# The mixer's second part: low parts, decay products and sums of squares on VectorE, weighted inputs and halos on ScalarE

## The chip, the cores and the metric

One core of a Trainium2 chip runs the whole program. The metric is the device time of one launch in microseconds. The engines are named as in the profile: PE is TensorE (PEld its weight loads), DVE is VectorE, ACT is ScalarE, POOL is GpSimd, SP issues the transfers.

## The reference

The program computes one block of a streaming encoder on 1024 tokens of width 1024, in float32: a conditioned RMS norm, a mixer that joins a 31-tap convolution path and a Mamba-2 path, a second conditioned norm, a SwiGLU layer, and a last norm. The part that the change touches is the Mamba-2 path with the products around it:

```python
xbc = jax.nn.silu(causal_depthwise_conv(xbc, ssm_conv_w, ssm_conv_b))      # 4 taps, 24 tiles of 128 channels
xs, bm, cm = jnp.split(xbc, [D_INNER, D_INNER + N_GROUPS * D_STATE], axis=-1)
dt = jax.nn.softplus(dt_raw + dt_bias);  a = -jnp.exp(a_log)
# scan over chunks, 32 heads in 4 groups; xk is xs * dt, ak is dt * a
acs = jnp.cumsum(ak, axis=1)
decay = jnp.exp(jnp.where(causal, acs[:, :, None] - acs[:, None, :], -jnp.inf))
cb = jnp.einsum("blgn,bsgn->blsg", ck, bk)
y_diag = jnp.einsum("blsg,blsgj,bsgjp->blgjp", cb, decay, xk)
y_off = jnp.einsum("blgn,bgjpn,blgj->blgjp", ck, state, jnp.exp(acs))
w_in = jnp.exp(last[:, None] - acs)
new_state = state * jnp.exp(last)[..., None, None] + jnp.einsum("bsgn,bsgj,bsgjp->bgjpn", bk, w_in, xk)
y = (y + d_skip * xs) * jax.nn.silu(z);  yg = yg * rsqrt(mean(yg * yg) + eps)
merged = sigmoid(g_conv) * y_conv + sigmoid(g_ssm) * (y @ w_ssm_out);  x = x + gate * (merged @ w_out)
```

## The kernel before

Activations lie as channels by tokens, in tiles of 128 channels by 512 tokens; the 1024 tokens are two halves, `hf` 0 and 1. TensorE multiplies at a format that keeps fewer bits, so each operand is split into a high part (a rounding copy, ScalarE) and a low part (the rest, a subtraction), and a product is three matmuls: high by high, high by low, low by high. A chunk of weights is 128 by 1024; `load_w` fetches it (512 KB, two buffers `wraw`), and `split_w` makes for each half of it the high part `wh` (L164, ScalarE) and the low part `wl` (L166). Which engine makes `wl` is the `eng` argument of `step`, "pool" (GpSimd) where nothing else is said; chunks are fetched three ahead and split two ahead of their use. `mm3` issues the three matmuls as L180, L181 and L182; only L182 reads `wl`.

The first part of the mixer (`phase_a`) and the SwiGLU layer work with seven products in place of eight on quarters of the operands (`Unit`); their own tables say which engine splits what, and they are not touched. The second part of the mixer (`phase_b`) runs from about 650 to 1450 us. In it, the main line is a list of steps, one chunk of weights each: 24 `group` steps (tiles `p`) whose result goes through the 4-tap convolution `conv4`, then gates, `conv_out` (`co`), `smul` (`s`) and `wout` (`wo`). `mm3` calls `tick`, which lets three background generators advance by given rates: `ssd_all` (the scan, for both halves and four groups), the end of the 31-tap convolution with its normalisation (`conv_var`, `conv_norm`), and `ada` (products of the conditioning vector, tiles `wa_m` and `wa_f`). A scheduler then sets the order on each engine from a timeline of its own and the priorities; every engine executes its list in that order, so what waits holds back all that stands behind it.

What the change touches:

- `SumSq` (L303 to L328) adds squares (made by ScalarE, L318) to an accumulator at L322; the engine is GpSimd where the caller names none. In `phase_b` these are `say` (the scan's groups), `sav` and `spare` (variance of the convolution, squares of the new residual).
- `dt_part` makes `wdec`, the decay from a token to the end of its chunk (L465 and L466), 128 tokens by 32 heads for each of four chunks.
- `ssd`: for each chunk four transposes give `px` in PSUM (tokens by 8 heads of 64); VectorE makes `xdt` from it by `dt` (L563), GpSimd makes the weighted inputs `wx` from `xdt` by `wdec` (L569); `next_state` multiplies `wx` on TensorE (L527) and VectorE adds the result to the scaled state (L531), whose scaling is GpSimd's (L522). `Decay` makes `M`, the decay within a chunk: loaded, four ScalarE instructions (L548), an exponential (L550), and the product with `cbm` (L553), which is GpSimd's for the first half and for every second head of the second, and VectorE's for the rest.
- `conv4` (L1081 to L1097) copies the product from PSUM into `pre` (L1088), scales it in place (L1090), adds three taps on VectorE (L1094), and ends with a tanh (L1096) and `xo` (L1097), which frees the PSUM tile. Three columns at the border of the halves are kept in `halo_s` (L1092) and put back in the second half (L1087), both by VectorE.
- `down_rest` names GpSimd for the sum of squares of the first half's output (L1552).

Of the kernel before, what the change touches and what calls it, by code (L numbers as in the profile page):

```python
# [15 lines left out]
T = 512  # L16
NH = 2
KD = 8
# [53 lines left out]
def build(tc, ins, outs):  # L72
# [230 lines left out]
    class SumSq:  # L303


        def __init__(self, name, square=True, eng=None, acc=None, of=None):
            self.name, self.n, self.square, self.eng = name, 0, square, eng or gp
            self.of, self.rest = of, []
            self.acc = acc if acc is not None else stp.tile([P, T], F32, tag="sacc", name="sa" + name, bufs=3)

# [91 lines left out]
    def dt_part(hf, wide, operands):  # L402
# [61 lines left out]
        act(out=etot, in_=pa[:, P:2 * P], func=AF.Exp)  # L464
        vec.tensor_tensor(out=wdec, in0=pa[:, P:2 * P], in1=acs, op=ALU.subtract)  # L465
        act(out=wdec, in_=wdec, func=AF.Exp)  # L466
        yield
        pt = pstile(f"acsT{hf}")
        for c in range(NCK):
# [16 lines left out]
    def ssd(hf, g, D):  # L486
# [47 lines left out]
        class Decay:  # L534
# [15 lines left out]
                act(out=m, in_=m, func=AF.Exp, scale=-1.0)  # L550

            def mul(self, e):
                (gp if e or hf == 0 else vec).tensor_tensor(out=self.M[e], in0=self.M[e], in1=cbm, op=ALU.mult)  # L553

        last = hf == NH - 1
        M = Decay(0)
# [1 line left out]
        for c in range(NCK):  # L558
            px = pstile(f"xT{hf}{g}{c}")
            for j in range(4):  # L560
                nc.tensor.transpose(out=px[:, j * P:(j + 1) * P], in_=xs[j][:, c * P:(c + 1) * P], identity=ident)
            xd = sp.tile([P, T], F32, tag="xdt", name=f"xdt{hf}{g}{c}", bufs=4)
            vec.tensor_tensor(out=v3(xd), in0=v3(px), in1=heads(dt, c, g), op=ALU.mult)  # L563
            xdt.append(xd)
            if c > 0:
                next_state(c - 1, sn)
            if not (last and c == NCK - 1):
                wx = sp.tile([P, T], F32, tag="wx", name=f"wx{hf}{g}{c}", bufs=2)
                gp.tensor_tensor(out=v3(wx), in0=v3(xd), in1=heads(wdec, c, g), op=ALU.mult)  # L569
                wxs.append(wx)  # L570
            if c == 0:
                M.load()
            elif c == 1:
                M.exp(0)
            elif c == 2:
                M.exp(1)
            else:
                M.mul(0)
                M.mul(1)
            yield 1  # L580
            if not (last and c == NCK - 1):
                sn = new_state(c)
            yield 1
# [179 lines left out]

    prog = []

    def step(fn, ch=None, nk=8, eng="pool", pre=()):
        prog.append((ch, nk, eng, fn, pre))

    W8 = list(range(8))
# [311 lines left out]
    def conv4(pt, i, out, hf):  # L1081

        pre = pools["c"].tile([P, T + SW - 1], F32, tag="pre", name=f"pre{hf}_{i}", bufs=2)
        if hf == 0:
            gp.memset(pre[:, 0:SW - 1], 0.0)
        else:
            vec.tensor_copy(out=pre[:, 0:SW - 1], in_=halo_s[:, i, :])  # L1087
        act(out=pre[:, SW - 1:], in_=pt, func=AF.Copy)  # L1088
        wc = lambda k: sw_h[:, i * SW + k:i * SW + k + 1]
        act(out=pt, in_=pt, func=AF.Identity, scale=wc(3), bias=sb_h[:, i:i + 1])  # L1090
        if hf == 0:
            vec.tensor_copy(out=halo_s[:, i, :], in_=pre[:, T:T + SW - 1])  # L1092
        for k in range(3):
            vec.scalar_tensor_tensor(out=pt, in0=pre[:, k:k + T], scalar=wc(k), in1=pt, op0=ALU.mult, op1=ALU.add)  # L1094
        t = pre[:, 0:T]
        act(out=t, in_=pt, func=AF.Tanh)  # L1096
        vec.scalar_tensor_tensor(out=out, in0=t, scalar=1.0, in1=pt, op0=ALU.add, op1=ALU.mult)  # L1097
# [437 lines left out]
    def down_rest(hf):  # L1535
# [11 lines left out]
        for m in range(KD):  # L1547
            def fd(w, m=m):
                pt = mmtile(f"fd{hf}_{m}")
                mm3(pt, w, range(6), LAST[hf])  # L1550
                if m == 0:
                    D["s"] = SumSq(f"x2_{hf}", eng=vec if hf else gp, of=KD)  # L1552
                    D["x2"] = []
                xt = (pools["u"].tile([P, T], F32, tag="g0", name=f"x2_{hf}_{m}", bufs=N_G0) if hf else
                      ev(f"x2_{hf}_{m}"))
# [198 lines left out]
```

## Time and profile before

| | |
|---|---|
| median of 3 runs | 2137.74 us (2136.13 to 2140.61) |
| the profiled execution, its own time | 2132.49 us |
| its span, first to last instruction | 2130.5 us |
| mean granted TensorE clock | 0.967 of full speed |
| busy: PE, DVE, ACT, POOL | 1954.8, 1561.3, 964.2, 1168.1 us |

The profiled execution is 5.25 us shorter than the median of the three runs; a sum made against its own time is carried to the median by adding that. Busy time of TensorE is the union of its matmuls; what it waits for, and in which stretch, says more than the share over the whole span.

### The profile page before, as it was taken

The numbers are of one execution on the slowest core, as the hardware profiler recorded it, in microseconds if no ns is written. First come the engines' busy times: TensorE is split into PE (matmuls) and PEld (weight loads), VectorE is DVE, ScalarE is ACT, GpSimd is POOL, SyncE is SP. The second block draws the span as 40 slices with busy tenths as digits, with TensorE's granted clock in tenths as the row PEclk, the third lists the DMA queues.
The fourth block names the chain that finished last, engine by engine and source line by source line (L and its number), as shares of the span: only waits on it lengthen the run. The fifth ranks groups of instructions, "written<-read, shape, count | busy, mean of one in ns | idle before, by whom it ended". The sixth has DMA issues, their size and how long they took to land.

```text
span 2130.5 us, 26723 instructions
## 1 busy us (share of the span) xinstructions
PE 1954.8 (92%) x8802; PEld 1554.5 (73%) x8802; DVE 1561.3 (73%) x2242; ACT 964.2 (45%) x1792; POOL 1168.1 (55%) x871
## 2 busy tenths in 40 slices
PE   4879999999998889898989899998999999989997
PEld 3668678787876666676767677776888888767776
DVE  8868889958899878959779783758644444598645
ACT  3534444444444747446344653346333333444243
POOL 4568678887885854585655764555333333331410
PEclk9889999999999989999999999999999999999998
DMA  8223132322323967689788786863422222576553
GB/s 321 80 70 113 68 102 84 119 104 74 109 102 135 302 201 247 201 301 290 242 277 271 246 260 218 275 229 109 149 99 77 77 84 89 180 255 215 190 187 119
DMA packets 163818, 365.94 MB, mean 172 GB/s; under 512 B 18728, under 2 KB 19168, under 8 KB 163680
## 3 DMA queue, kind: packets, MB, share of 16 engines
q1 hardware_dynamic: 163680, 364.25, 51.2%
q8 instruction: 69, 1.13, 0.2%
q14 instruction: 69, 0.57, 0.1%
HBM read 281.04 MB, written 83.13 MB: 171 GB/s over the span
## 4 chain that ended last, share of the span: by engine, by line
PE 53%; DVE 23%; DMA 13%; issue 4%; ACT 3%; POOL 3%; SPq 1%; DVEq 0%; POOLq 0%; ACTq 0%
PE uXp L805 12%; PE uXf L805 10%; PE uZp L805 6%; PE uZf L805 5%; PE uYp L805 3%; PE uYf L805 2%; DMA M<-acs_d 2%; PE uXd L805 2%; DMA wa_f<-in 2%; DMA yl<-y_d 1%; DVE wa_m L242 1%; DVE wa_f L242 1%; DVE Hl L211 1%; PE uZd L805 1%; PE fd L180 1%
## 5 line engine op out<-in xcount | busy, mean ns | idle before, releaser
L166 POOL TENSOR_TENSOR wl<-w,wh 128x512 fp32r<-128x512 f32 x198 | 283.4, 1440 | 226.6 <-ACT wh L164 185.6
L164 ACT ACTIVATE wh<-w 128x512 fp32r<-128x512 f32 x232 | 136.8, 606 | 135.4 <-DMA w<-in 60.1
L918 POOL TENSOR_TENSOR fw<-fw,fw 128x512 f32<-128x512 f32 x40 | 58.0, 1450 | 117.5 <-DMA fw<-in 116.8
L548 ACT ACTIVATE M<-M,dt_acs 128x128 f32<-128x128 f32 x256 | 81.0, 390 | 45.2 <-DMA M<-acs_d 45.0
L553 POOL TENSOR_TENSOR M<-M,cbm 128x512 f32<-128x512 f32 x48 | 69.4, 1456 | 44.4 <-ACT M L550 25.9
L660 DVE SCALAR_TENSOR_TENSOR pcM<-u,cw_eo,pcM 128x512 f32<-128x512 f32 x120 | 90.3, 752 | 2.7
L660 DVE SCALAR_TENSOR_TENSOR pcQ<-u,pc,pcQ 128x512 f32<-128x512 f32 x112 | 84.4, 754 | 3.0
L182 PE MATMUL s<-Hh,wl 128*128 128x512 f32 x192 | 77.8, 406 | 3.0 <-POOL wl L166 3.0
L660 DVE SCALAR_TENSOR_TENSOR pcR<-u,pc,pcR 128x512 f32<-128x512 f32 x104 | 78.4, 754 | 2.8
L181 PE MATMUL s<-Hl,wh 128*128 128x512 f32 x192 | 77.1, 401 | 2.5 <-DVE Hl L211 2.5
L180 PE MATMUL s<-Hh,wh 128*128 128x512 f32 x192 | 77.3, 406 | 0.5 <-ACT wh L164 0.5
L916 POOL TENSOR_TENSOR fsf<-fw 128x512 f32<-128x512 f32 x22 | 41.2, 1873 | 65.3 <-DVE cf2l L784 10.8
L180 PE MATMUL p<-Hh,wh 128*128 128x512 f32 x144 | 59.0, 430 | 19.1 <-DVE xo L1097 10.8
L180 PE MATMUL p<-Oh,wh 128*128 128x512 f32 x144 | 60.6, 421 | 8.4 <-DVE xo L1097 8.4
L181 PE MATMUL p<-Hl,wh 128*128 128x512 f32 x144 | 60.7, 423 | 5.9 <-DVE Hl L341 5.9
L985 DVE TENSOR_TENSOR s2f<-s2f,uZf 128x512 f32<-128x512 f32 x22 | 15.1, 687 | 62.5 <-PE uZf L805 62.5
L181 PE MATMUL p<-Ol,wh 128*128 128x512 f32 x144 | 60.0, 417 | 0.0
L182 PE MATMUL p<-Oh,wl 128*128 128x512 f32 x144 | 59.5, 414 | 0.0
L925 POOL TENSOR_TENSOR fw<-fw 128x512 f32<-128x512 f32 x40 | 58.6, 1466 | 1.5
L182 PE MATMUL p<-Hh,wl 128*128 128x512 f32 x136 | 56.8, 418 | 0.0
L1094 DVE SCALAR_TENSOR_TENSOR p<-pre,pc,p 128x512 f32<-128x512 f32 x72 | 53.9, 748 | 0.8 <-ACT p L1090 0.2
L180 PE MATMUL wo<-Oh,wh 128*128 128x512 f32 x128 | 51.6, 403 | 0.0
(3620 smaller groups left out, 6973.7 us busy)
## 6 DMA issues: line engine op xcount, KB each, us to landing
fw<-in SPq DMA_DIRECT2D x133, 512.0 KB, 3.4
w<-in SPq DMA_DIRECT2D x100, 512.0 KB, 4.9
M<-acs_d SPq DMA_DIRECT2D x64, 256.0 KB, 6.1
wa_f<-in SPq DMA_DIRECT2D x48, 256.0 KB, 3.5
wa_m<-in SPq DMA_DIRECT2D x16, 512.0 KB, 10.2
xs<-xbc_d SPq DMA_DIRECT2D x32, 256.0 KB, 5.0
E<-eac_d SPq DMA_DIRECT2D x64, 128.0 KB, 6.1
y<-z_d SPq DMA_DIRECT2D x32, 256.0 KB, 5.2
```

Source lines behind the costliest of these rows:

```text
L164: act(out=hi[:, :n], in_=raw, func=AF.Copy)
L166: eng.tensor_tensor(out=lo[:, :n], in0=raw, in1=hi[:, :n].bitcast(F32), op=ALU.subtract)
L180: nc.tensor.matmul(out=out, lhsT=whi[:, sl], rhs=rh, start=first and i == 0, stop=False)
L181: nc.tensor.matmul(out=out, lhsT=whi[:, sl], rhs=rl, start=False, stop=False)
L182: nc.tensor.matmul(out=out, lhsT=wlo[:, sl], rhs=rh, start=False, stop=last and i == n - 1)
L548: act(out=m[:, sl], in_=m[:, sl], func=AF.Relu, scale=-1.0, bias=acs[:, c * 32 + hd:c * 32 + hd + 1])
L553: (gp if e or hf == 0 else vec).tensor_tensor(out=self.M[e], in0=self.M[e], in1=cbm, op=ALU.mult)
L660: vec.scalar_tensor_tensor(out=pt if k < n - 1 else out or pt, in0=src(k), scalar=w(k), in1=pt, op0=ALU.mult, op1=ALU.add)
L805: nc.tensor.matmul(out=out, lhsT=l[:, sl], rhs=r, start=first and k == 0 and i == 0, stop=k == 3 and i == 2, skip_group_check=True)
L918: e[8].tensor_tensor(out=a21, in0=a11, in1=a21, op=ALU.subtract)
L925: e[10].tensor_tensor(out=a12, in0=a12, in1=a11, op=ALU.subtract)
L1094: vec.scalar_tensor_tensor(out=pt, in0=pre[:, k:k + T], scalar=wc(k), in1=pt, op0=ALU.mult, op1=ALU.add)
```

## The change

Five edits, all of them of who does what; one adds a small product.

1. `step` gives `wl` to VectorE where nothing else is said (188 low parts in the stretch 650 to 1450 us, and those of the two gate chunks near the start, which go through the same default).
2. `Decay.mul` is VectorE's for all 64 tiles (48 of them were GpSimd's).
3. `SumSq` adds on VectorE where no engine is named, and `down_rest` names none.
4. `wx` is made by ScalarE, straight from `px` in PSUM, in eight instructions of 64 columns with the decay as a scale for each partition; `wdec` is multiplied by `dt` once for each half beforehand, since `px` lacks it.
5. The two halo copies of `conv4` are ScalarE's.

```diff
-            self.name, self.n, self.square, self.eng = name, 0, square, eng or gp
+            self.name, self.n, self.square, self.eng = name, 0, square, eng or vec
...
         act(out=wdec, in_=wdec, func=AF.Exp)
+
+        vec.tensor_tensor(out=wdec, in0=wdec, in1=dt, op=ALU.mult)
...
-                (gp if e or hf == 0 else vec).tensor_tensor(out=self.M[e], in0=self.M[e], in1=cbm, op=ALU.mult)
+                vec.tensor_tensor(out=self.M[e], in0=self.M[e], in1=cbm, op=ALU.mult)
...
-                gp.tensor_tensor(out=v3(wx), in0=v3(xd), in1=heads(wdec, c, g), op=ALU.mult)
+                for h in range(J):
+                    hs = slice(h * 64, (h + 1) * 64)
+                    o = c * 32 + g * J + h
+                    act(out=wx[:, hs], in_=px[:, hs], func=AF.Copy, scale=wdec[:, o:o + 1])
...
-    def step(fn, ch=None, nk=8, eng="pool", pre=()):
+    def step(fn, ch=None, nk=8, eng="vec", pre=()):
...
-            vec.tensor_copy(out=pre[:, 0:SW - 1], in_=halo_s[:, i, :])
+            act(out=pre[:, 0:SW - 1], in_=halo_s[:, i, :], func=AF.Copy)
...
-            vec.tensor_copy(out=halo_s[:, i, :], in_=pre[:, T:T + SW - 1])
+            act(out=halo_s[:, i, :], in_=pre[:, T:T + SW - 1], func=AF.Copy)
...
-                    D["s"] = SumSq(f"x2_{hf}", eng=vec if hf else gp, of=KD)
+                    D["s"] = SumSq(f"x2_{hf}", of=KD)
```

Two places show what the scheduler makes of it. The first is on VectorE, at the second chunk `p_21` of the first half's group 2: from its last tap to its `xo`, in the kernel before (`xh_x1m`, `Ol` belong to the next half's normalised input, `ud` to the convolution's variance, `yd` to the scan).

```order
L1094 SCALAR_TENSOR_TENSOR p_21_5999<-pre_22_6052,pc,p_21_5999 128x512
L709 TENSOR_TENSOR ud_7_5762<-ud_7_5762,bcmean_5268 128x512
L1092 COPY halo_s<-pre_8_6130 128x3
L335 SCALAR_TENSOR_TENSOR xh_x1m_5987<-xh_x1m_5987,gmix,bcx1m 128x512
L1094 SCALAR_TENSOR_TENSOR p_22_6078<-pre_8_6130,pc,p_22_6078 128x512
L335 SCALAR_TENSOR_TENSOR xh_x1m_6066<-xh_x1m_6066,gmix,bcx1m 128x512
L335 SCALAR_TENSOR_TENSOR xh_x1m_6144<-xh_x1m_6144,gmix,bcx1m 128x512
L1094 SCALAR_TENSOR_TENSOR p_22_6078<-pre_8_6130,pc,p_22_6078 128x512
L613 SCALAR_TENSOR_TENSOR yd_5907<-xs_2_5372,pc,yd_5907 128x512
L1097 SCALAR_TENSOR_TENSOR xo_6051<-pre_22_6052,p_21_5999 128x512
```

The same place in the changed kernel (its lines stand five further down, L1099 for the taps and L1102 for `xo`; L555 is the product `M`).

```order
L1099 SCALAR_TENSOR_TENSOR p_21_6028<-pre_22_6081,pc,p_21_6028 128x512
L335 SCALAR_TENSOR_TENSOR xh_x1m_6173<-xh_x1m_6173,gmix,bcx1m 128x512
L268 TENSOR_SCALAR vv_5984<-scv_5979 128x4
L606 TENSOR_TENSOR E_6034<-E_6034,yo_6039 128x384
L322 TENSOR_TENSOR say_5675<-say_5675,sqy_1_5877 128x512
L1099 SCALAR_TENSOR_TENSOR p_22_6107<-pre_8_6159,pc,p_22_6107 128x512
L341 SCALAR_TENSOR_TENSOR Ol_5324<-xh_x1m_6016,mod_m,Oh_5323 128x512
L621 TENSOR_TENSOR yd_5936<-E_5888,yd_5936 128x384
L341 SCALAR_TENSOR_TENSOR Ol_5326<-xh_x1m_6095,mod_m,Oh_5325 128x512
L269 TENSOR_SCALAR r_ln_126<-vv_5984 128x4
L166 TENSOR_TENSOR wl_0_6296<-w_6175,wh_0_6294 128x512
L1102 SCALAR_TENSOR_TENSOR xo_6080<-pre_22_6081,p_21_6028 128x512
```

The low part, the sum `say` and the work of the scan now stand between a tap and the `xo` that TensorE waits for. From the chunk's first tap to its `xo` there were 19 other rows on VectorE; now there are 30. From its second tap there were 14; now there are 23.

The second place is the weighted inputs at the start of the scan's first group. On GpSimd they stood, in the kernel before, among low parts and products `M`:

```order
L569 TENSOR_TENSOR wx_5487<-xdt_5482,dt_wdec_2162 128x512
L553 TENSOR_TENSOR M_5447<-M_5447,cbm_5400 128x512
L1085 MEMSET pre_7_5872 128x3
L166 TENSOR_TENSOR wl_4_5813<-w_5707,wh_4_5811 128x512
L553 TENSOR_TENSOR M_5449<-M_5449,cbm_5400 128x512
L166 TENSOR_TENSOR wl_0_5892<-w_5805,wh_0_5890 128x512
```

On ScalarE they stand, in the changed kernel, between the steps of `conv4` (L1093 and L1095 are its copy and its scaling, L1101 its tanh) and the high parts of weights:

```order
L1097 ACTIVATE halo_s<-pre_6_5818 128x3
L164 ACTIVATE wh_0_5919<-w_5834 128x512
L574 ACTIVATE wx_5558<-xT_5548,dt_wdec_2162 128x64 x8
L552 ACTIVATE M_5697<-M_5697 128x512
L164 ACTIVATE wh_4_5923<-w_5834 128x512
L1101 ACTIVATE pre_6_5818<-p_14_5746 128x512
L574 ACTIVATE wx_5603<-xT_5593,dt_wdec_2162 128x64 x8
L1093 ACTIVATE pre_7_5901<-p_15_5844 128x512
```

A block of eight now stands ahead of a tanh, a copy or a high part, where ScalarE had nothing of the kind; GpSimd keeps the scaling of the state and little else in this stretch.

## Rows read from the trace of the kernel before

**Rows 1.** The page, part 1: busy us (share of span) and instructions.

```profile
PE 1954.8 (92%) x8802; PEld 1554.5 (73%) x8802; DVE 1561.3 (73%) x2242; ACT 964.2 (45%) x1792; POOL 1168.1 (55%) x871
```

**Rows 2.** Three stretches: their us, busy us by engine, clock, DMA share, GB/s.

```profile
650.00:900.00 250.00, 216.80 (x1082) 167.51 (x1080) 213.43 (x343) 149.13 (x308) 147.68 (x122) 0.93 0.68 221
900.00:1250.00 350.00, 316.00 (x1656) 246.90 (x1655) 279.85 (x433) 184.13 (x409) 225.68 (x164) 0.96 0.83 273
1250.00:1450.00 200.00, 192.04 (x849) 152.45 (x848) 118.06 (x175) 76.93 (x136) 98.84 (x71) 1.00 0.74 245
```

**Rows 3.** Waits of PE, 650 to 1450 us: total us, times, longest.

```profile
PE p L180 <- DVE xo L1097: 19.2, 3, 10.8
PE yo L596 <- DVE S L531: 8.5, 4, 3.4
PE yd L611 <- POOL M L553: 6.8, 6, 3.6
PE sc L285 <- DVE ry L276: 6.5, 2, 3.5
PE yo L596 <- DVE E L601: 5.6, 3, 3.8
...
PE s L182 <- POOL wl L166: 3.8, 6, 1.2
```

**Rows 4.** Groups on POOL, 650 to 1450 us: busy, mean ns, idle before.

```profile
L166 POOL TENSOR_TENSOR wl<-w,wh 128x512 fp32r<-128x512 f32 x188 | 269.1, 1440 | 198.7 <-ACT wh L164 169.4 <-PE s L182 11.3 <-DMA y_d<-y 9.0
L553 POOL TENSOR_TENSOR M<-M,cbm 128x512 f32<-128x512 f32 x48 | 69.4, 1456 | 44.4 <-ACT M L550 25.9 <-DMA wa_f<-in 12.4 <-DMA E<-eac_d 3.9
L322 POOL TENSOR_TENSOR say<-say,sqy 128x512 f32<-128x512 f32 x24 | 33.5, 1397 | 9.2 <-ACT sqy L318 8.9
L569 POOL TENSOR_TENSOR wx<-xdt,dt_wdec 128x512 f32<-128x512 f32 x28 | 31.3, 1123 | 2.6 <-DVE xdt L563 2.6
```

**Rows 5.** Groups on DVE, 650 to 1450 us.

```profile
L242 DVE CUSTOM_DVE_ANT_0 wa_f<-wa_f,rw,as_f 128x512 f32<-128x512 f32 x24 | 29.0, 1209 | 30.1 <-DMA wa_f<-in 30.1
...
L563 DVE TENSOR_TENSOR xdt<-xT,dt_dt 128x512 f32<-128x512 f32 x32 | 21.2, 681 | 2.9 <-PE xT L561 2.9
...
L1289 DVE TENSOR_TENSOR spl<-spl,mpl 128x512 f32<-128x512 f32 x16 | 18.8, 1177 | 0.3
...
L274 DVE SCALAR_TENSOR_TENSOR ty<-ry 128x4 f32<-128x4 f32 x24 | 11.2, 466 | 0.5
...
L1092 DVE COPY halo_s<-pre 128x3 f32<-128x3 f32 x12 | 5.3, 438 | 6.2 <-ACT pre L1088 6.2
...
L274 DVE SCALAR_TENSOR_TENSOR tv<-r_ln 128x4 f32<-128x4 f32 x6 | 0.9, 155 | 0.0
```

**Rows 6.** Timeline of DVE, then of POOL, 737 to 753 us: start, us, what.

```profile
738.83 0.74 DVE L1094 SCALAR_TENSOR_TENSOR p<-pre,pc,p 128x512 f32<-128x512 f32 x1
...
741.56 2.41 DVE L341 SCALAR_TENSOR_TENSOR Ol<-xh_x1m,mod_m,Oh 128x512 fp32r<-128x512 f32 x2
...
752.12 0.68 DVE L1097 SCALAR_TENSOR_TENSOR xo<-pre,p 128x512 f32<-128x512 f32 x1
752.72 0.75 DVE L1094 SCALAR_TENSOR_TENSOR p<-pre,pc,p 128x512 f32<-128x512 f32 x1
...
741.68 1.75 POOL L322 TENSOR_TENSOR sav<-sav,sqv 128x512 f32<-128x512 f32 x1
743.39 1.71 POOL L553 TENSOR_TENSOR M<-M,cbm 128x512 f32<-128x512 f32 x1
```

**Rows 7.** Groups on ACT, 650 to 1450 us.

```profile
L548 ACT ACTIVATE M<-M,dt_acs 128x128 f32<-128x128 f32 x256 | 81.0, 390 | 45.2 <-DMA M<-acs_d 45.0
L550 ACT ACTIVATE M<-M 128x512 f32<-128x512 f32 x64 | 38.3, 618 | 0.0
```

**Rows 8.** Low parts: POOL's wait, 650 to 1450 us; VectorE's at the end, 1990 to 2131 us.

```profile
POOL wl L166 <- ACT wh L164: 169.4, 72, 7.6
...
L166 DVE TENSOR_TENSOR wl<-w,wh 128x512 fp32r<-128x512 f32 x16 | 11.1, 691 | 25.8 <-ACT wh L164 25.8
```

## The prediction

> **What bounds the kernel now.** I read the page's first part, then the stretches, then what TensorE waits for in the changed part, then the groups of VectorE and GpSimd there. Over the span TensorE is busy 92%, VectorE 73%, GpSimd 55% [rows 1]: no engine but TensorE could set the end by its own sum. The change lies in 650 to 1450 us, apart from four low parts near the start and six sums near the end. In these 800 us TensorE is busy 216.8 + 316.0 + 192.0 = 724.8 us, so it stands 75.2 us; its clock is at 0.93 and 0.96 of full speed in the first two stretches [rows 2]. VectorE is busy 611.3 us of the 800 (85%, 80%, 59% by stretch), GpSimd 472.2, ScalarE 410.2. What ends TensorE's waits is mostly VectorE: `xo` 19.2 us, the state 8.5, the small root chain `ry` 6.5, `E` 5.6, together 39.8; GpSimd ends 6.8 (`M`) and 3.8 (`wl`), 10.6 in all [rows 3]. So the first 250 us are bound by VectorE and TensorE in turn, the last 200 by TensorE with the supply of weights, and more than 75 us, with what a higher clock adds, cannot be won here.
>
> **Why VectorE is so busy.** An instruction of VectorE that reads PSUM takes 681 ns (`xdt`), whoever runs beside it; one of the same size that reads two tiles from SBUF has a mean of 1177 (L1289) and one with 4 columns 466 against 155 in another group of the same instruction [rows 5]. The timeline shows why: two such instructions take 2.41 us from 741.56, while GpSimd's start at 741.68 and 743.39 and take 1.75 and 1.71; the two engines go in step, one waiting for the other [rows 6]. The Trainium skill says it outright ("SBUF — State Buffer", Who interferes with whom): a VectorE instruction with two SBUF inputs and a GpSimd one that reads SBUF exclude each other, for a whole instruction. These rows agree.
>
> **What leaves VectorE.** In the view by group, 29 groups of VectorE without a PSUM operand are longer than their free time, from `wa_f` (24 times 1209 ns) to the halo copy L1092 (12 times 438) [rows 5]. I take as free time 690 ns for 512 columns, 745 where a scale for each partition or a running sum goes with it, and 155 for four columns or fewer, and the two halo groups whole since they leave: group by group, the count times the excess comes to 139 us. Nearly all goes if GpSimd is silent, and it nearly is: `wl`, `M`, `say` and `wx` are 403 us of its 472 [rows 4], 27 further sums like `say` some 38 (an estimate from its 1397 ns), which leaves about 31.
>
> **What VectorE gets.** 188 low parts, 48 products and 24 + 27 sums are 287 instructions. One takes 0.69 us [rows 8], but from start to start it is 0.60 (752.12 to 752.72) [rows 6], so 172 us. Two products for `wdec` are below 1 us. Net: 611 - 139 + 172 = 644 us, 81% in place of 76%. So VectorE's load hardly changes; what changes is that no single instruction takes 1.7 us, and that GpSimd is out of the chain. At the first place of the changed order this is nearly even: from the second tap of `p_21` to its `xo`, 16 instructions took 738.83 to 752.80, 13.97 us [rows 6]. Now 25 stand there, two of them with four columns; the other 23 at 0.605 are 13.9 us. The 10.8 us for which TensorE waited for this `xo` [rows 3] do not shrink there.
>
> **What ScalarE gets.** 28 tiles `wx` [rows 4] of eight instructions are 224. 128 columns with a scalar for each partition take 81.0/256 = 0.316 us back to back; from 390 to 618 ns over 384 columns [rows 7], 64 columns less are 0.038 less, so 0.278 each and 62 us in all (54 with no columns at all, 71 at the row's price). With 24 halo copies at about 0.24, ScalarE goes from 410 to 478 of 800 us, 60%. A tile takes 2.2 us against 1.1 on GpSimd, but starts from PSUM without the wait for `xdt` and behind no queue of low parts. If all of the difference were exposed, it would be 28 x 1.1 = 31 us; TensorE's wait for `wx` is under 1 us now, and the state is fetched a step later, so I take 1. A rule speaks against this edit: the Trainium skill ("ScalarE: Activation LUTs", Rules for kernel authors) wants a plain multiply on VectorE. By it VectorE would get 28 x 0.6 = 17 us more and ScalarE 62 less; by its page's fixed cost (an estimate) the 224 would be 54 us. With ScalarE at 60% and VectorE at 81%, the rows give the rule no force here.
>
> **What the new order costs.** A low part waits for its high part from ScalarE. GpSimd spent 169.4 us in 72 such waits [rows 8], at no cost, since little stood behind. On VectorE the taps, `xo` and the scan stand behind. At the program's end VectorE already makes low parts for 16 chunks, and waits 25.8 us for the first halves of them [rows 8]: 1.6 us a chunk, or 152 us for 94 chunks. That is the upper end, from a place where VectorE has little else; the lower is nothing, if the scheduler puts each behind its high part. I take 0.15 us a part, 28 us of waiting; VectorE has 800 - 644 = 156 us to spare, so I let a fifth reach TensorE: 5 us. Slack helps: chunks are split two ahead of their use, and TensorE waits 3.8 us in all for 188 parts made in 1.44 us each.
>
> **The sum**, in TensorE's waits. `M` and `wl`: 10.6, of which a quarter stays for VectorE's queue: -8. The root chains, a dozen small instructions that may each take 0.47 on the mean and 0.155 alone: more than half of 6.5, -4. State and `E`, 14.1, shorter by a third as their VectorE instructions meet no neighbour: -5. `xo`: 10.8 stay, of 8.4 a third goes: -3. The clock of the first stretch, 0.93, rises a little when waits go: -2. Against it +5 and +1. Net -16: 2132.5 - 16 = 2116.5 for the profiled execution, and with its 5.25 us to the median, **2121.7 us**. The thirds and the fifth are chosen; ends -8 and -30. The four low parts at the start (4 x 0.6 = 2.4 us on a busy VectorE, less what GpSimd's four no longer block) and the six sums of the tail, where VectorE stands often, I set to nothing, within 3 us either way.
>
> **The rivals.**
> (a) *More comes off.* If the blocked instructions were the ones that TensorE waits for, half of its 39.8 us on VectorE goes, GpSimd's 10.6 go whole, and the clock of the first stretches recovers by 0.03 of 533 us, 16: -46, or about 2092. For it: `xo`'s longest wait falls into the stretch where the engines go in step. Against: the place above, where the moved work takes what the blocking gives.
> (b) *An even swap.* VectorE's load stays, so its waits stay, and GpSimd's 10.6 return as queueing: 2134 to 2142, no difference. The Trainium skill ("Perfetto Trace Analysis", Optimizing Scalar/DVE Operations) warns that moving work between these two engines might not help because they share a port. For it: 644 against 611. The rows bear that out in part: what leaves the shared reads is 1.44 us a piece, what comes is 0.60. That, and the shorter single instruction, speak against it.
> (c) *Slower: VectorE held by high parts.* The stretch is as long as VectorE's work and waits, divided by how full it can be; the fullest stretch now is 85% [rows 2]. 0.85 x 800 = 680 us, so 36 us of new waits, 0.19 us a part, is the point from which VectorE decides. At 0.25 us, 47 us, the stretch is (644 + 47)/0.85 = 813, +13: a median of 2151. My own 0.15 lies close below, and 1.6 a chunk was seen; ScalarE is also later by 68 us of work in the same line as those high parts. Against: the scheduler can put a low part late, and slack is several matmuls.
>
> **How the numbers follow.** Forecast 0.43 (2108 to 2133 is its own range), (a) 0.16, (b) 0.16, (c) 0.25. About 0.2%, 4.3 us, is what a measurement of this kernel can tell from no change. Faster 0.43 + 0.16 = 0.59, less 0.01 for its upper edge; same 0.16; slower 0.26. Range 2088 to 2150: it takes in (b), most of (a) and the first half of (c).
>
> **What would show it.** Right: GpSimd near 30 us busy in 650 to 1450; two-input instructions of VectorE (L1289, `Hl`, `un`) near 690 ns; VectorE at 630 to 660 us there; ScalarE near 478; the new `wx` at 0.25 to 0.35 us each; TensorE's waits for GpSimd gone and for VectorE below 35; TensorE idle below 65 us. Wrong, if VectorE waits over 40 us for `wh`, if TensorE waits more than now for `xo` (19.2) or `wl` (3.8), or if VectorE's instructions stay at 1.1 us with GpSimd silent.

## The result, and the profile after

| | before | after |
|---|---|---|
| median of the runs | 2137.3 us (2136.13 to 2140.61, 4 runs) | 2116.98 us (2115.29 to 2121.91, 4 runs) |
| the profiled execution, its own time | 2132.49 us | 2117.58 us |
| its span | 2130.5 us | 2115.9 us |

The ratio is 0.9906, with a 95% interval of 0.9889 to 0.9923: faster by about 20 us in the medians, by 14.9 us in the two profiled executions, which are the pair that the traces can account for. The forecast was 2121.7.

Part 1 of the profile's page for the changed kernel answers to [rows 1]: GpSimd lost 446 us of work, VectorE gained 35, ScalarE 50, TensorE's own sum fell by 2.8.

```profile
PE 1952.0 (92%) x8802; PEld 1553.6 (73%) x8802; DVE 1596.1 (75%) x2517; ACT 1013.7 (48%) x2040; POOL 721.6 (34%) x546
```

The three stretches of [rows 2], in the changed kernel:

```profile
650.00:900.00 250.00, 219.47 (x1054) 171.25 (x1055) 212.94 (x408) 165.31 (x405) 12.07 (x20) 0.92 0.69 224
900.00:1250.00 350.00, 317.38 (x1696) 244.41 (x1696) 296.12 (x561) 212.94 (x559) 20.30 (x17) 0.96 0.83 267
1250.00:1450.00 200.00, 197.86 (x881) 161.52 (x880) 141.41 (x256) 86.98 (x148) 10.19 (x7) 1.00 0.75 255
```

VectorE does 1225 instructions in these 800 us where it did 951, in 650.5 us where it took 611.3. Its groups in 640 to 1440 us show why that is no more (columns: busy us, mean ns of one, idle before it and what ended that):

```profile
L166 DVE TENSOR_TENSOR wl<-w,wh 128x512 fp32r<-128x512 f32 x188 | 132.8, 711 | 17.2 <-ACT wh L164 16.9
...
L555 DVE TENSOR_TENSOR M<-M,cbm 128x512 f32<-128x512 f32 x64 | 43.2, 699 | 12.3 <-ACT M L552 12.1
...
L1294 DVE TENSOR_TENSOR spl<-spl,mpl 128x512 f32<-128x512 f32 x16 | 11.5, 717 | 1.9 <-DMA mpl<-mp_d 1.7
...
L726 DVE TENSOR_TENSOR Hl<-un,Hh 128x512 fp32r<-128x512 f32 x16 | 10.9, 684 | 0.0
...
L274 DVE SCALAR_TENSOR_TENSOR ty<-ry 128x4 f32<-128x4 f32 x24 | 5.7, 237 | 0.2
```

The third row is L1289 of [rows 5], 1177 ns there and 717 here; the four-column L274 fell from 466 to 237. What TensorE waits for in 640 to 1440 us, beside [rows 3]:

```profile
PE p L180 <- DVE xo L1102: 22.3, 7, 7.7
PE xT L563 <- DMA xs<-xbc_d: 7.6, 3, 5.2
PE co L180 <- ACT Hh L740: 4.7, 2, 2.4
PE yo L601 <- DVE S L533: 3.9, 1, 3.9
PE yd L616 <- DVE M L555: 3.4, 3, 2.6
PE s L180 <- DVE xo L1102: 3.2, 2, 2.4
...
PE p L182 <- DVE wl L166: 1.9, 2, 1.4
...
PE st L529 <- ACT wx L574: 1.6, 2, 0.8
```

No wait for GpSimd is left, and the states and `E` are down, but `xo` is up: 22.3 + 3.2 = 25.5 us.

**Where the 14.6 us of the span lie.** The mixer's second part is taken from here on as the stretch from the last matmul of its first part (`uXp`) to the last `wo`. It holds the same 3405 or 3406 matmuls in every kernel, so its length splits into TensorE busy and TensorE standing. Before, it is this row of the view by stretches, and after, the next one:

```profile
668.50:1426.10 757.60, 685.73 (x3406) 535.66 (x3405) 578.16 (x894) 388.03 (x816) 459.07 (x346) 0.96 0.77 252
```

```profile
664.80:1413.70 748.90, 685.73 (x3405) 537.07 (x3404) 608.10 (x1157) 437.86 (x1065) 30.36 (x35) 0.95 0.78 255
```

TensorE stood 71.9 us and now 63.2: 8.7 us won, all of it standing time. Up to the first `uXp` the program went from 87.4 to 84.0 us, 2.9 of the 3.4 us in TensorE's busy time (49.4 to 46.5 for 184 and 185 matmuls, at a granted clock of 0.92 and 0.98). The first part proper gave 0.3, what follows the second part 2.2.

### The profile page after: what moved, and what is told of

It is laid out like the page before. It is cut to its first block, busy times and chain, and to the rows that moved or that the text cites. A ratio compares the mean times of both kernels' runs of the same rounds, so it can differ in the third digit from the quotient of the medians.

```text
span 2115.9 us, 26745 instructions
## 1 busy us (share of the span) xinstructions
PE 1952.0 (92%) x8802; PEld 1553.6 (73%) x8802; DVE 1596.1 (75%) x2517; ACT 1013.7 (48%) x2040; POOL 721.6 (34%) x546
## 4 chain that ended last, share of the span: by engine, by line
PE 59%; DVE 18%; DMA 12%; issue 5%; ACT 4%; POOL 2%; SPq 1%; DVEq 0%; ACTq 0%; POOLq 0%
PE uXp L810 11%; PE uXf L810 10%; PE uZp L810 6%; PE uZf L810 5%; PE uYp L810 3%; PE uXd L810 2%; PE s L181 2%; DMA M<-acs_d 2%; PE uYf L810 2%; PE s L182 2%; PE s L180 2%; DMA w<-in 1%; PE p L180 1%; PE p L181 1%; PE uZd L810 1%
## 5 line engine op out<-in xcount | busy, mean ns | idle before, releaser
L166 DVE TENSOR_TENSOR wl<-w,wh 128x512 fp32r<-128x512 f32 x224 | 153.2, 688 | 38.5 <-ACT wh L164 34.0
L524 POOL TENSOR_TENSOR S<-S,dt_etot 128x512 f32<-128x512 f32 x16 | 18.7, 1169 | 329.7 <-ACT S L531 166.2
L838 POOL TENSOR_TENSOR b<-Hh,Hl 128x512 f32<-128x512 f32 x8 | 11.9, 1495 | 223.5 <-DVE spare L322 196.7
L990 DVE TENSOR_TENSOR s2f<-s2f,uZf 128x512 f32<-128x512 f32 x22 | 15.1, 686 | 62.5 <-PE uZf L810 62.5
L182 PE MATMUL p<-Hh,wl 128*128 128x512 f32 x136 | 56.7, 417 | 0.0
L180 PE MATMUL co<-Hh,wh 128*128 128x512 f32 x128 | 51.5, 414 | 5.1 <-ACT Hh L740 4.7
```

Of the source, the lines that this page charges most:

```text
L166: eng.tensor_tensor(out=lo[:, :n], in0=raw, in1=hi[:, :n].bitcast(F32), op=ALU.subtract)
L180: nc.tensor.matmul(out=out, lhsT=whi[:, sl], rhs=rh, start=first and i == 0, stop=False)
L182: nc.tensor.matmul(out=out, lhsT=wlo[:, sl], rhs=rh, start=False, stop=last and i == n - 1)
L524: gp.tensor_tensor(out=v3(sn), in0=v3(S[c]), in1=heads(etot, c, g), op=ALU.mult)
```

## The experiments

Each kernel was timed beside the kernel before on the same chip. Three theories are named in the expectations. A: VectorE's work stays level because GpSimd no longer lengthens its instructions, and what is won is hand-overs and long single instructions. B: an even swap in the mixer, with the gain from the start and a lucky order. C: the gain is `wx` on ScalarE. "Excess" is what VectorE's instructions on shared operands last beyond 760 ns for 512 columns (560 for 384, 160 for four), summed over 650 to 1450 us: 138 us before, 17 after.

**1. One part alone, three times** (each is the kernel before with one part of the diff).

```diff
# e1_low: edit 1
-    def step(fn, ch=None, nk=8, eng="pool", pre=()):
+    def step(fn, ch=None, nk=8, eng="vec", pre=()):
# e2_msum: edits 2 and 3 (Decay.mul; SumSq and down_rest are left out here)
-                (gp if e or hf == 0 else vec).tensor_tensor(out=self.M[e], in0=self.M[e], in1=cbm, op=ALU.mult)
+                vec.tensor_tensor(out=self.M[e], in0=self.M[e], in1=cbm, op=ALU.mult)
...
# e3_act: edits 4 and 5 (wx; the product for wdec and the halos are left out here)
-                gp.tensor_tensor(out=v3(wx), in0=v3(xd), in1=heads(wdec, c, g), op=ALU.mult)
+                for h in range(J):
+                    hs = slice(h * 64, (h + 1) * 64)
+                    o = c * 32 + g * J + h
+                    act(out=wx[:, hs], in_=px[:, hs], func=AF.Copy, scale=wdec[:, o:o + 1])
...
```

> The kernel before with the low parts alone on VectorE. Theory A (VectorE's work stays level because GpSimd no longer blocks it, and what is won is short instructions and GpSimd's hand-overs): GpSimd keeps some 200 us of its 472 in 650 to 1450 us, the excess of VectorE's two-input instructions falls from 138 to about 60 us, and about half of the 20 us is won: 2127 us. Rival B (the moved work costs as much as the blocking, and the gain comes from the start and from a lucky order): the start wins its 4 us, the stretch nothing or a loss: 2130 to 2142 us. Rival C (the gain is the weighted inputs on ScalarE, which shorten the chain of the state): as before, 2137, or slower.

> The kernel before with the products M and the sums of squares alone on VectorE. Theory A: 131 us of GpSimd's work leave the stretch, the excess falls by about 40 us to 100, VectorE gets 60 us: a small gain, about 2132 us. Rival B: 2135 to 2142. Rival C: 2137.

> The kernel before with the weighted inputs and the halos alone on ScalarE. Theory A: 31 of GpSimd's 472 us leave, ScalarE gets about 68 us: no difference, 2133 to 2141 us. Rival C: most of the gain, 2118 to 2125 us.

Measured: low parts alone 2126.75 us (0.995, 0.993 to 0.997), `M` and sums alone 2128.93 (0.9958, 0.9935 to 0.9982), the ScalarE part alone 2150.54 (1.007, 1.0046 to 1.0093). C falls: the part that it rests on costs time by itself. The second part of the mixer in these three, in that order:

```profile
664.80:1423.80 759.00, 688.70 (x3406) 537.33 (x3405) 613.40 (x1080) 390.70 (x816) 206.61 (x160) 0.96 0.78 252
```

```profile
663.80:1414.80 751.00, 681.61 (x3406) 534.63 (x3405) 602.59 (x992) 389.17 (x816) 330.06 (x248) 0.97 0.78 254
```

```profile
670.00:1442.30 772.30, 689.82 (x3405) 538.72 (x3404) 562.72 (x871) 434.47 (x1064) 429.19 (x318) 0.95 0.77 248
```

TensorE stands 70.3, 69.4 and 82.5 us, against 71.9 before. Neither of the first two removes standing time worth the name in this part, though the excess fell to 75 and 109 us. Of the 5.6 us by which the profiled span of the first is shorter, 3.3 come after this part and none in TensorE's busy time (0.7 us more over the span); of the 8.7 us of the second, 6.3 are TensorE's busy time, so the granted clock. In the first, TensorE now waits for the two things that GpSimd still makes:

```profile
PE st L527 <- POOL wx L569: 4.8, 4, 1.9
...
PE yd L611 <- POOL M L553: 3.8, 3, 2.2
```

In the second it waits for `wx` behind GpSimd's low parts, and for VectorE's `M`:

```profile
PE yd L611 <- DVE M L553: 13.0, 8, 6.5
...
PE st L527 <- POOL wx L569: 4.6, 2, 3.1
```

All waits of TensorE for GpSimd in the second part come to 12.4 us before, 10.4 with the low parts alone, 7.5 with `M` and sums alone: part of the wait moves to what GpSimd still has. With the low parts alone that is not the largest shift, though: waits for VectorE fell by 9.9 us, and waits that end at ScalarE rose by 11.8. In the third, ScalarE's row for `wx` says what it waits for:

```profile
L574 ACT ACTIVATE wx<-xT,dt_wdec 128x64 f32<-128x64 f32 x224 | 49.1, 346 | 30.9 <-DVE xdt L565 30.9
```

`xdt` is VectorE's other reader of the same PSUM tile. ScalarE stood 30.9 us for it, with high parts and `conv4` queued behind, and TensorE's longest wait for `xo` became 16.2 us.

**2. The low parts of the gate chunks back on GpSimd** (the changed kernel otherwise).

```diff
-            step(f, CH_GC + m)
+            step(f, CH_GC + m, eng="pool")
```

> The changed kernel with the four low parts of the two gate chunks near the start back on GpSimd, nothing else. If the 4 us by which the end of the first part comes earlier in the changed kernel are due to these four: 2121 us, and the first product of the first part starts at 87 us in place of 84. If they are not: 2117 us, at 84.

Measured 2123.52 us (0.9933, 0.9909 to 0.9956), first `uXp` at 86.0 us, last at 669.0 where the changed kernel has 664.8. It looked like 4 us for four low parts. Other runs took that back: in run 1's second kernel, which also has them on GpSimd, the first `uXp` came at 85.8 us and the last at 663.8. Over all runs but the one with additions near the start (run 6), the first `uXp` came at 84.0 to 86.0 us with these parts on VectorE and at 85.8 to 87.7 with them on GpSimd. What the start gives is not shown.

**3. The whole change without its ScalarE part, and without `wx` on ScalarE alone.**

```diff
# e8_no_act, against the changed kernel: wx as in the kernel before; no product for wdec and halos on VectorE are left out here
-                for h in range(J):
-                    hs = slice(h * 64, (h + 1) * 64)
-                    o = c * 32 + g * J + h
-                    act(out=wx[:, hs], in_=px[:, hs], func=AF.Copy, scale=wdec[:, o:o + 1])
+                gp.tensor_tensor(out=v3(wx), in0=v3(xd), in1=heads(wdec, c, g), op=ALU.mult)
...
# e6_wx_gp: the same, but the halos stay on ScalarE
```

> The whole change without its ScalarE part: low parts, M and the sums of squares on VectorE, but wx and the weights on GpSimd and the halos on VectorE as before. The three parts alone gave -12.2, -10.0 and +11.5 us, which sum to -10.7 against -20.3 for all of them together, so they are not additive and this run closes the square. If the ScalarE part costs in company what it cost alone, this one is some 11 us faster than the changed kernel: 2104 to 2108. If the cost was VectorE's lateness with xdt (ScalarE idled 30.9 us on it alone and 11.5 in company), which the other two parts cure, the part is about neutral here: 2114 to 2120. If it helps in company, as theory C would have it, 2121 or more. Theory A (what counts is what GpSimd still does beside VectorE) says GpSimd busy in 650 to 1450 near 190 us (wx, wdec and say), VectorE's excess 35 to 60 us, against 17 in the changed kernel and 75 with the low parts alone, and so 2120 to 2126. Theory B (an even swap) has no number of its own here: 2110 to 2128.

> The changed kernel with wx back on GpSimd from xdt and the weights unscaled; the halos stay on ScalarE. It tells wx from the halos within the ScalarE part. Theory A: GpSimd has about 150 us more in the mixer's second part, VectorE's excess rises from 17 to 35 to 60 us, and the time by 2 to 6 us: 2119 to 2123. If wx on ScalarE is what costs in the run of that part alone (its wait behind xdt), 2106 to 2112. The halos by themselves are priced at under 1 us, so this run and the one without the whole ScalarE part should be within 3 us of each other.

Measured 2112.39 us (0.9888, 0.9874 to 0.9903) and 2114.24 (0.9895, 0.9881 to 0.9908). The second part of the first:

```profile
665.10:1409.90 744.80, 681.06 (x3406) 534.25 (x3405) 620.18 (x1180) 390.11 (x818) 64.92 (x63) 0.96 0.79 257
```

TensorE stands 63.7 us there and 60.4 in the other, as in the changed kernel (63.2). So the ScalarE part takes no standing time away, and the two moves to VectorE, worth 1.6 and 2.5 us of it apart, are worth 8.2 together. That the pair does more than its halves is not shown by this: six kernels with both moves differ among themselves by 3.5 us in standing, and a seventh, with `wx` turned round (run 4), by 11 from the least of them; and in time the halves add up, since 0.995 times 0.9958 is 0.991, against 0.9888 and 0.9895 with overlapping intervals. The 4.7 us in busy time between this row and the changed kernel's are the clock's. The numbers that A gave for these runs were wrong: GpSimd is busy 80 us in 650 to 1450 where A said 190 (I had counted `say` in, which has moved), the excess is 32 and 23, and neither is slower for it.

**4. `wx` ahead of `xdt`**, so that VectorE waits for ScalarE: the `wx` block of the changed kernel moves above the `xdt` line, and so also above the update of the state of the chunk before, which stood between the two.

```diff
-            vec.tensor_tensor(out=v3(xd), in0=v3(px), in1=heads(dt, c, g), op=ALU.mult)
-            xdt.append(xd)
-            if c > 0:
-                next_state(c - 1, sn)
...
                     act(out=wx[:, hs], in_=px[:, hs], func=AF.Copy, scale=wdec[:, o:o + 1])
                 wxs.append(wx)
+            vec.tensor_tensor(out=v3(xd), in0=v3(px), in1=heads(dt, c, g), op=ALU.mult)
+            xdt.append(xd)
+            if c > 0:
+                next_state(c - 1, sn)
```

> The changed kernel with wx emitted ahead of xdt in each chunk, so that the wait between the two readers of the PSUM tile is turned round: wx waits for TensorE alone, and VectorE's xdt waits for the fourth of wx's pieces. The changed kernel has ScalarE idle 11.5 us on xdt. If that wait is on the path, the time falls by 2 to 6 us (2111 to 2115); if VectorE is the engine to spare, its xdt now stands behind some 1.3 to 2.2 us of ScalarE's work in each of 56 chunks, VectorE idles 30 to 100 us more in the stretch, and the time rises by 3 to 15 us (2120 to 2132). Theory A leans to the second, since VectorE is the busier of the two by 650 to 465 us.

Measured 2122.52 us (0.9933, 0.9915 to 0.9951), an interval that overlaps the changed kernel's. The chunks with a `wx` are 28, not 56. TensorE stands 71.1 us in the second part, 8 more than in the changed kernel, and 61.1 us of its waits are for VectorE (45.9 in the changed kernel). The direct price is small, though:

```profile
DVE xdt L572 <- ACT wx L570: 1.5, 3, 0.9
```

So the standing rose, but the path by which it did is not shown, and this is one order.

**5. Reads by GpSimd beside VectorE's work.** The changed kernel with one GpSimd addition per low part, which reads `wh`. It writes into `t1f[3]`, which is not idle as I had thought: it holds a tile of the normalised input of the SwiGLU layer, so that part of that layer's input is overwritten.

```diff
             act(out=hi[:, :n], in_=raw, func=AF.Copy)
             lo = alloc("wlo", f"wl{ch}_{q}")
             eng.tensor_tensor(out=lo[:, :n], in0=raw, in1=hi[:, :n].bitcast(F32), op=ALU.subtract)
+            if "b" in pools:
+                gp.tensor_tensor(out=t1f[3], in0=hi.bitcast(F32), in1=rw[:, 64:64 + T], op=ALU.add)
```

> The changed kernel with 188 extra GpSimd operations of 128 x 512, one ahead of each low part in the mixer's second part, which read the weight tile and write into a tile that no one reads; no engine waits for them. It puts GpSimd's load back (some 150 to 350 us in the stretch) without any hand-over. Theory A holds that GpSimd's work beside VectorE's lengthens VectorE's: the excess goes from 17 us to 80 to 140, and the time up by 4 to 12 us (2121 to 2129). Theory B holds that only the hand-overs and their order counted: excess below 40 us, time within 3 us of the changed kernel (2114 to 2120).

Measured 2199.27 us (1.0289, 1.0265 to 1.0313), 82 us above the changed kernel where A expected 4 to 12. The second part, and the group of the additions:

```profile
667.00:1497.50 830.50, 710.63 (x3406) 550.89 (x3405) 728.54 (x1155) 437.10 (x1062) 315.26 (x218) 0.93 0.71 230
```

```profile
L168 POOL TENSOR_TENSOR t1f<-wh,rw 128x512 f32<-128x512 f32 x188 | 291.7, 1552 | 459.2 <-ACT wh L164 439.1 <-ACT bry L289 4.7 <-ACT pre L1094 3.2
```

No wait of TensorE ends at GpSimd; ScalarE waits 4.5 us for the additions to leave `wh`. But VectorE is 120 us busier with the same instructions (excess 123 us), full to 728.5/830.5 = 88%. TensorE stands 56.7 us more: it waits 93.9 us for VectorE in place of 45.9, 24.6 for ScalarE in place of 8.6, and 7.6 less for transfers. The other 24.9 of the 82 us are busy time at a lower clock (710.6 us against 685.7, at 0.93 of full speed and not 0.95). `S` is scaled on GpSimd behind these additions, in a queue that waits for `wh`, but little of the delay is a hand-over of it: VectorE waits 0.3 us in all for GpSimd in this part.

**6. GpSimd additions that hang on nothing**, to have no hand-over at all.

```diff
+    waste = hpool.tile([P, 192], F32, name="waste")
...
                 gp.tensor_tensor(out=v3(sn), in0=v3(S[c]), in1=heads(etot, c, g), op=ALU.mult)
+                if c == NCK - 1 - hf:
+                    for _ in range(30):
+                        gp.tensor_tensor(out=waste, in0=rw[:, 64:256], in1=rw[:, 320:512], op=ALU.add)
```

> The changed kernel with 30 extra GpSimd additions of 128 x 192, two reads of the row constants and a write into a tile of its own, behind the last state scaling of each of the 8 groups in the mixer's second part and the 8 in its first: no engine waits for them, they wait for nothing but GpSimd's own queue, and the next scaling is due 15 to 90 us later. Unlike the run with extra reads of the weight tile, nothing is handed over. Some 110 us more of GpSimd's time in 650 to 1450. Theory A: VectorE's instructions beside them get longer, the excess over 760 ns rises from 17 to 40 to 70 us, and the time by 2 to 7 us (2119 to 2124). Theory B: VectorE's lengths stay as they are (excess below 25 us) and the time within 3 us of the changed kernel.

Measured 2169.98 us (1.0147, 1.0121 to 1.0174), and it missed its aim. What hangs on nothing is put early: the scheduler set most of the 240 into the first part, where GpSimd has little to spare. The last `uXp` came at 712.7 us (664.8), and from there to the last `wo` it took 751.9 us (748.9). Only 10 of the additions ran in the second part, so it tests neither theory there. Up to the last `uXp`, where the other 230 ran, it does speak against B: VectorE was busy 610.9 us there, against 563.4 in the changed kernel. Of its additions, subtractions and multiply-adds with 512 columns, the 209 that ran beside an extra addition for 0.1 us or more had a mean of 983 ns, and the 48 beside nothing of GpSimd 727. Whether the longer first part came from VectorE or from GpSimd's own queue (634 us busy of 713) is not shown.

**7. The changed kernel again, and in another order.**

```diff
# e9_rate
-SSD_RATE = 0.85
+SSD_RATE = 0.84
```

> The changed kernel once more, unchanged, beside the three others and on their chip. The four runs before it put the kernel without the ScalarE part at 0.9888 of the kernel before and the changed one at 0.9906, on different chips. All theories: 2115 to 2119 and a ratio of 0.989 to 0.992. If it comes out below 0.989, the ScalarE part costs nothing in company.

> The changed kernel with the number that paces the mixer's steps at 0.84 for 0.85 (SSD_RATE): the same instructions on the same engines, some hundreds of them in another order. It tells how much of any difference between two kernels here is the order alone. Theory A, which explains 14 us by loads and lengths, needs the order to be worth less than 4 us: 2113 to 2121. Theory B, in which a lucky order gives the gain, would not wonder at 2121 to 2130.

Measured 2121.15 us (0.9918, 0.9892 to 0.9945) and 2126.5 (0.9942, 0.9924 to 0.9961). The same kernel's second profile has a span of 2121.4 us, 5.5 more than its first, and its page says in which sum:

```profile
PE 1959.7 (92%) x8802; PEld 1559.6 (74%) x8802; DVE 1596.5 (75%) x2517; ACT 1015.0 (48%) x2040; POOL 721.3 (34%) x546
```

TensorE is 7.7 us busier over the same 8802 matmuls and stands 161.7 us where it stood 163.9. So these two executions of one kernel differ by the clock, while the standing time repeats within some 2 us: for this kernel it is the better meter, on the evidence of one pair. In the second part it is 63.1 us in the repeat and 63.9 in the other order. Medians of these two differ by 5 us with overlapping intervals: no edit here worth less than that has been told from the order by its time alone, and the run does not decide about A's limit of 4 us for the order, although its 2126.5 lies outside A's range and inside B's.

**8. The sums of squares back on GpSimd too**, in the kernel of run 3 without the ScalarE part.

```diff
-        sq = SumSq(f"y{hf}{g}")
+        sq = SumSq(f"y{hf}{g}", eng=gp)
```

> The kernel without the ScalarE part, with the mixer's sums of squares (24 additions of 128 x 512 in the stretch) back on GpSimd as well, where wx and the weights are; low parts, M and the second part's other sums stay on VectorE. VectorE is spared some 17 us, GpSimd gets some 30 us, and the norm after each group waits for GpSimd again. Theory A counts GpSimd's 30 us against it (some 10 us more excess) and the hand-over in the norm's chain (before, 24 additions on GpSimd), so 2113 to 2120 and not faster than without it; if VectorE's own load is what counts, 2106 to 2111.

Measured 2114.01 us (0.9889, 0.9862 to 0.9916): no difference from 2112.39, in time or in standing (63.8 us). It can stay on either engine.

**All of them side by side.** The second part of the mixer, in us, with TE for TensorE; the waits of TensorE in it are the rows of the view of waits, added up by the engine (or DMA) that ended them.

| kernel | ratio to before | length | TE busy | TE stands | for VectorE | GpSimd | ScalarE | DMA |
|---|---|---|---|---|---|---|---|---|
| before | 1 | 757.6 | 685.7 | 71.9 | 52.3 | 12.4 | 3.3 | 3.6 |
| low parts alone | 0.995 | 759.0 | 688.7 | 70.3 | 42.4 | 10.4 | 15.1 | 1.8 |
| `M`, sums alone | 0.9958 | 751.0 | 681.6 | 69.4 | 53.9 | 7.5 | 5.1 | 2.9 |
| ScalarE part alone | 1.007 | 772.3 | 689.8 | 82.5 | 54.3 | 8.2 | 12.7 | 3.4 |
| changed kernel | 0.9906 | 748.9 | 685.7 | 63.2 | 45.9 | 0 | 8.6 | 8.3 |
| the same again | 0.9918 | 752.4 | 689.3 | 63.1 | 45.2 | 0 | 10.2 | 7.6 |
| gate chunks on GpSimd | 0.9933 | 750.5 | 689.2 | 61.3 | 40.2 | 0 | 8.2 | 12.4 |
| another order | 0.9942 | 753.6 | 689.7 | 63.9 | 43.6 | 0 | 12.2 | 7.6 |
| no ScalarE part | 0.9888 | 744.8 | 681.1 | 63.7 | 55.2 | 1.2 | 1.1 | 5.8 |
| `wx` on GpSimd | 0.9895 | 748.5 | 688.1 | 60.4 | 46.0 | 2.4 | 9.7 | 1.9 |
| sums on GpSimd too (run 8) | 0.9889 | 747.0 | 683.2 | 63.8 | 54.1 | 4.7 | 0.5 | 3.9 |
| `wx` before `xdt` | 0.9933 | 756.3 | 685.2 | 71.1 | 61.1 | 0 | 8.9 | 0.6 |
| reads added | 1.0289 | 830.5 | 710.6 | 119.9 | 93.9 | 0 | 24.6 | 0.7 |
| free additions (run 6) | 1.0147 | 751.9 | 682.7 | 69.2 | 41.6 | 2.5 | 21.8 | 2.9 |

## Why the prediction was right, and where it was not

The sign and the size held: 2117.58 against 2116.5 for the profiled execution, 2116.98 against 2121.7 for the median. The size held partly by luck. The -16 was a sum of TensorE's waits in the mixer's second part and its clock there; in that part TensorE's standing fell by 8.7 us and its busy time not at all, and 5.6 of the 14.6 us came before the first `uXp` and after the last `wo`, where nothing was forecast. Within the sum, terms that were off cancelled.

- **VectorE's level: right.** 650.5 us against 644, two-input instructions (the groups above) at 684 to 717 ns against the 690 forecast, the excess 17 us of 138 (the prediction's 139 counts from shorter free times). The extra reads (run 5) show the same mechanism backwards. Over additions, subtractions and multiply-adds with 512 columns in 650 to 1450 us, counted by their overlap with GpSimd's instructions: before, 300 that overlapped by 0.4 us or more had a mean of 931 ns and 200 with no overlap 710; after, 44 have 939 and 795 have 700. `xdt`, which reads PSUM, was not lengthened: 30 of its 32 instructions before ran beside GpSimd's and took 674 to 692 ns. These rows agree with the Trainium skill's rule ("SBUF — State Buffer", Who interferes with whom), that the ports which the two engines share are an exclusive lock, and that a VectorE instruction with two SBUF inputs contends there with a GpSimd instruction that reads SBUF.
- **What that is worth: not shown as I had put it.** I took time from each chain for its shorter instructions. But low parts alone took 63 us of the excess away and 1.6 us of TensorE's standing. The hand-over fits better, without being shown: 12.4 us of waits for GpSimd before, 10.4 or 7.5 while one of the two kinds of work stayed there, 1.2 and 2.4 with both moves (run 3), which take 8.2 and 11.5 us of standing. Against it as the whole account, `wx` before `xdt` has no wait for GpSimd and stands 71.1 us, and run 8 has 4.7 us of them and stands 63.8. Which wait carries the gain stays open. Rival (b) falls all the same, and B with it: the six kernels that have both moves, and neither turn `wx` round nor add instructions to GpSimd, stand 60.4 to 63.9 us (61.3 in run 2), where before stood 71.9.
- **The terms.** `M` and `wl`: -8 forecast; the rows went from 6.8 + 3.8 to 3.4 + 1.9, so -5.3. State and `E`: -5 forecast; the rows of the state and `E`, 14.1, are down to 3.9 and 0.2, -10. Root chains: -4 forecast, 6.5 to 0.3, -6.2. The clock: -2 forecast, in the second part nothing (685.7 both times). `wl` waiting for `wh` on VectorE: 28 us forecast, 16.9 measured, 0.09 us a part.
- **`xo`: the step that failed.** The prediction took 3 us off 19.2 and said that 10.8 stay at `p_21`, because the way from its second tap to its `xo` stays as long on VectorE. It does: 13.9 us forecast, 14.29 measured, from 742.72 to 757.01 in the changed kernel:

```profile
742.72 0.75 DVE L1099 SCALAR_TENSOR_TENSOR p<-pre,pc,p 128x512 f32<-128x512 f32 x1
...
756.33 0.68 DVE L1102 SCALAR_TENSOR_TENSOR xo<-pre,p 128x512 f32<-128x512 f32 x1
```

  But TensorE no longer stands there. The two stretches, before and after (columns of [rows 2]):

```profile
738.83:752.80 13.97, 1.97 (x14) 1.56 (x14) 13.97 (x18) 7.05 (x13) 10.84 (x7) 0.50 0.64 215
```

```profile
742.72:757.01 14.29, 14.09 (x70) 11.46 (x69) 14.29 (x27) 12.94 (x29) 0.10 (x1) 0.69 0.77 241
```

  In the new order TensorE has other products to make meanwhile. Elsewhere waits for `xo` came, 25.5 us in all: TensorE stood 7.7 us from 677.2 and 6.7 from 850.4. I had written that more than 19.2 would prove it wrong, and for this step it does. At 677.2 this is VectorE in the changed kernel, its `xo` behind an instruction that waits for a transfer and one that waits for ScalarE:

```profile
681.46 1.29 DVE L714 TENSOR_TENSOR ud<-ud,bcmean 128x512 f32<-128x512 f32 x2 [2.32 <-DMA bcmean<-row_d]
683.45 0.69 DVE L322 TENSOR_TENSOR sav<-sav,sqv 128x512 f32<-128x512 f32 x1 [0.69 <-ACT sqv L318]
684.06 1.28 DVE L1102 SCALAR_TENSOR_TENSOR xo<-pre,p 128x512 f32<-128x512 f32 x2
```

  ScalarE's `wx` is not the reason for these two: run 3's kernels, with `wx` on GpSimd, stand 7.4 and 7.6 us at the first place and 6.5 and 4.2 at the second. With the low parts alone TensorE stands 6.5 us at the first (put down to ScalarE's `sqv`, which ended within 0.1 us of the first of these `xo`), before and with `M` and sums alone 2.8 us (put down to the tanh ahead of the `xo`), so the rise came with the low parts. Over all places the two kernels have 15.0 and 15.8 us; the other 10 us of the changed kernel may be `wx`'s (argued, not shown: each order is one sample).
- **`wx`: dearer in the forecast than measured, and its wait wrong.** 224 instructions took 48.9 us, below the range (62 forecast, 54 to 71), with a mean of 350 ns that overlaps the next one's start. "Starts from PSUM without the wait for `xdt`" was false. The changed kernel's row, beside the 30.9 us of run 1:

```profile
L574 ACT ACTIVATE wx<-xT,dt_wdec 128x64 f32<-128x64 f32 x224 | 48.9, 350 | 11.5 <-DVE xdt L565 11.5
```

  Two engines read one PSUM tile here, and the program keeps them apart with a wait, so `wx` comes after `xdt` as it did on GpSimd. I could have known: the Trainium skill ("PSUM — Partial Sum Buffer", PSUM bank collisions raise a hardware error) says that two engines must not access the same bank and quadrant of partitions at once, reads included, and that the compiler's scheduler puts a dependency between them. No run here shows a collision; the wait is in the row above.
- **Start and tail: 0 within 3 us forecast**; 3.4 us came before the first `uXp`, nearly all of it clock, and 2.2 after the last `wo`, 5.6 together. The same kernel again has 2.3 and 1.4.
- **Signs that did not come.** TensorE's waits for VectorE were to fall below 35 us and are 45.9. TensorE was to be idle below 65 us in 650 to 1450 and is 65.3, and GpSimd is busy 42.6 us there, where 30 were named.
- **Rival (c) has its point, but elsewhere (argued).** It said that VectorE decides from 85% of the stretch on. The changed kernel is at 608.1/748.9 = 81% and gains, the one without the ScalarE part at 83%; with the added reads it is at 88% and loses 82 us. What filled it there was GpSimd, not the waits for high parts.

**What stays open.** Whether the three kernels without `wx` on ScalarE (0.9888, 0.9889, 0.9895) really beat the changed one (0.9906 and 0.9918): the intervals overlap, and their traces don't agree on where a difference would lie. Over the profiled spans, the first two have TensorE 3.6 and 5.1 us less busy than the changed kernel, and standing 1.9 and 3.1 less; the third has it 5.9 us busier, and standing 8.1 less. Why the clock differs the runs don't tell. Of the 20 us between the medians, the traces account for the 14.6 of the profiled pair. `wx` on VectorE, as the rule that the prediction weighed ("ScalarE: Activation LUTs" of the Trainium skill, Rules for kernel authors: a plain multiply belongs there) would have it, was not run.

## What to carry to other kernels

Judge a move off a helper engine by all the waits of the bounding engine, not by the row that it aims at: each of two moves off GpSimd alone took 1.6 or 2.5 us from TensorE's standing in the stretch, since other rows grew, and both together took 8.2. The helper need not be emptied: with 30 to 100 us of work left on GpSimd there, six kernels with both moves stand 60 to 64 us alike. That an engine's work keeps its length does not tell whether TensorE waits for it; ask what TensorE has to do meanwhile. Before a second engine reads the same PSUM tile as a first, look in the program for the wait between the two readers, and price it. Compare variants by how long the bounding engine stands over a stretch with the same number of its instructions: in the one pair of executions here that repeats within 2 us, while the span moves by 5.5.

## What I had not expected of the hardware

GpSimd's reads cost much beside a VectorE that is 81% busy: 292 us of additions for which other engines waited 4.8 us in all made VectorE 120 us busier, and the second part 82 us longer. And ScalarE's eight pieces of 64 columns from PSUM, with means of 346 and 350 ns, take 48.9/224 = 0.22 us of its busy time each, less than the 0.28 that I had drawn from the 128-column group of [rows 7].
